# Convolution tail of a two-layer diffusion step: first chunk's norm between the other means, last adaLN group around it, second chunk's norm among the pointwise products

## The chip, the cores and the metric

The kernel runs on one core of one Trainium2 chip. The metric is the device time of one execution in microseconds (us). A core has five engines that run side by side, each through its own list of instructions in order: TensorE (PE; PEld is its weight load), VectorE (DVE), ScalarE (ACT), GpSimd (POOL) and SyncE (SP), which here issues nearly all transfers. An instruction that waits holds up all that stand behind it on its engine.

## The reference

One step of a hybrid backbone for 128 context tokens and 1024 noisy tokens, 1024 channels, two layers. Layer 0 mixes tokens by a convolution, layer 1 by attention; each is followed by a convolutional FFN.

```python
mod = (silu(cond) @ ada_w[i] + ada_b[i])                    # adaLN, per layer
sh1, sc1, g1, sh2, sc2, g2 = split(mod, 6)
h = modulate(rmsnorm(x, norm1_g[i]), sh1, sc1)
# layer 0, conformer_conv:
a, g = split(h @ w_pw1, 2);  u = a * sigmoid(g)
u = dwconv(u, dw_w, dw_b)                                   # 31 taps per channel
u = silu(layernorm(u, ln_g, ln_b))
y = u @ w_pw2
x = x + g1 * y
h = modulate(rmsnorm(x, norm2_g[i]), sh2, sc2)
x = x + g2 * conv_ffn(h, ...)
```

All is float32; each large product is made of three, with weights and activations split into a high and a low part.

## The kernel before

Channels lie on partitions, in 8 tiles (`KT`) of 128; the 1152 tokens lie along the free axis, in three chunks of 384 columns (`NCH`, index `c`). Only the stretch around the change is told here.

**Gate products and taps.** `gated(j, c)` makes channel tile `j` of the convolution's input `u`: two products (`ppa`, `ppg`) of 24 matmuls, a sigmoid, a multiplication. For tiles 0 to 6 the 31 taps are shared between VectorE (`taps_vector`, into the PSUM tile `da`) and ScalarE with GpSimd (`taps_pool`, into `pacc`); `join` adds the two into `U[c][:, j]`. For the last tile, `j = 7`, TensorE does 16 taps of each chunk with diagonal matrices (`taps_tensor`, into `dl`), VectorE adds seven more (`L660`) and GpSimd's eight join them (`L666`).

**Norm of a chunk.** `mean_head(c)` adds channel tiles 0 to 6 into the mean `mu` (seven matmuls, `L737`). `layer_norm(c)` is a generator, advanced a step at a time: the last matmul of the mean (`L744`), which needs the join of tile 7; two subtractions on VectorE (`L749`); squares on ScalarE (`lnsq`), summed on VectorE and GpSimd (`lnss`); six small matmuls that sum them over channels (`lnv`, `L325`); the reciprocal root on GpSimd (`lnv_r`); three matmuls that spread it over partitions (`L342`); then multiplications, SiLU and the split into `ln_h` and `ln_l`. `mu` of chunks 1 and 2, the norms' banks, `dl` and the products share PSUM tiles.

**adaLN.** `ada(pool, l, grp)` is a generator too. It reads 2048 columns of `ada_w` in 16 transfers of 512 KB ("halves" below, two to a step), each into one of three buffers `adaw`, and multiplies each by `cs` (`L270`, two matmuls of 512 columns that a trace shows as four). A row to SBUF by ScalarE (`adar`, `L279`), four transposes (`adat`) and additions into `mods` end a group. Group (1, 2) is the last of six; its result is not read before layer 1.

**Products.** `project_residual` runs for `c` = 0, 1, 2 over eight output tiles `m`: a product `pw2p` of 24 matmuls with weight tile `w16`, `w17`, ..., the residual on VectorE into `X[c]` (`L384`), a square on ScalarE. `X[c]` is read back from DRAM (`reload`, `L388`) into the buffer that `U[c]` held, so the transfer starts when the last `ln_l` of that chunk is written. `weights` keeps three raw tiles in flight and splits each on ScalarE (`w_hi`, `L220`) and VectorE (`w_lo`, `L221`).

**Order.** A scheduler orders the instructions of each engine, except where `manual_schedule` names an engine: there program order holds. SP is in program order everywhere. Before, VectorE and TensorE are in program order from the taps of tile 6 up to the end of the loop over the last taps, and the generators in `bg` (the adaLN groups, then the norms) advance one step per `tick()`.

Of the kernel before, what the change touches and what calls it, by code (L numbers as in the profile page):

```python
# [18 lines left out]
KT = D // P  # L19
# [4 lines left out]
NCH = NT // CH  # L24
# [55 lines left out]
def tile_hybrid_step(ctx: ExitStack, tc: tile.TileContext, a: dict, outs: list):  # L80
# [31 lines left out]
    def ntile(name, n=CH, dt=F32):  # L112
        return np_.tile([P, n], dt, tag="n", name=name)
# [30 lines left out]
    pool = Banks()  # L144


    bg = []

    def tick():
        for g in list(bg):  # L150
            if next(g, "end") == "end":
                bg.remove(g)
# [90 lines left out]
    weights = Weights()  # L243
# [8 lines left out]
    def ada(pool, l, grp):  # L252
        def load(kt):
            out = []
            for half in range(2):
                w = slot("adaw", f"adaw{l}_{grp}_{kt}_{half}")
                c0 = grp * 2048 + half * 1024
                nc.sync.dma_start(w, a["ada_w"][l, kt * P : (kt + 1) * P, c0 : c0 + 1024])
                out.append(w)
            return out  # L260

        nxt = load(0)
        yield
        ps = pool("ms", f"ada{l}_{grp}")
        for kt in range(KT):
            w = nxt
            if kt + 1 < KT:
                nxt = load(kt + 1)
            for q in range(4):
                nc.tensor.matmul(  # L270
                    ps[32 * q : 32 * q + 32, :],
                    cs[:, kt, :],
                    w[q // 2][:, (q % 2) * 512 : (q % 2) * 512 + 512],
                    start=(kt == 0),
                    stop=(kt == KT - 1),
                )
            yield
        row = slot("adaw", f"adar{l}_{grp}", n=512)
        nc.scalar.activation(row, ps, AF.Copy)  # L279
        yield  # L280
        pt = pool("ms", f"adat{l}_{grp}")
        for i in range(4):
            nc.tensor.transpose(pt[:, i * P : (i + 1) * P], row[:, i * P : (i + 1) * P], ident)
        ptv = pt.rearrange("p (i q c) -> p q i c", i=4, c=32)
        b0 = grp * 16
        for cond in range(2):
            nc.vector.tensor_tensor(
                mods[l][:, b0 : b0 + 16, cond].rearrange("p (q i) -> p q i", i=4),
                ptv[:, :, :, cond],
                adab[:, l * 48 + b0 : l * 48 + b0 + 16].rearrange("p (q i) -> p q i", i=4),  # L290
                ALU.add,
            )
        for n, gname in ((0, "norm1_g"), (1, "norm2_g")):
            v = 1 + 3 * n
            if v // 2 == grp:
                for cond in range(2):
                    nc.vector.scalar_tensor_tensor(
                        gsc[l][n][:, :, cond],
                        mods[l][:, v * 8 : v * 8 + 8, cond],
                        1.0,  # L300
                        cols(gname, l * KT, KT),
                        ALU.add,
                        ALU.mult,
                    )
# [172 lines left out]
    def chain(*gens):  # L477
        for g in gens:
            yield from g
# [25 lines left out]
    def cols(name, i, n):  # L505
        return vecs[:, at[name] + i : at[name] + i + n]
# [3 lines left out]
    slot = lambda tag, *args, **kw: (slot_0 if tag in ("adaw", "vrow") else slot_a)(tag, *args, **kw)  # L510
# [68 lines left out]
    us = []  # L579

    def gated(j, c):

        if c == 0:
            us.append((weights.take(min(j, 1)), weights.take(min(j, 1)), slot("u", f"u{j}")))
            for z in (0, NS + HALF, NT + 2 * HALF):
                nc.gpsimd.memset(us[j][2][:, z : z + HALF], 0.0)
        wa, wg, u = us[j]
        psa = project(pool, wa, H[c], f"ppa{j}_{c}")
        tick()
        psg = project(pool, wg, H[c], f"ppg{j}_{c}")  # L590
        yield
        tick()
        sg = ntile(f"sg{j}_{c}")
        nc.scalar.activation(sg, psg[:, 0:CH], AF.Sigmoid)
        for lo, hi, cond in pieces(c):
            o = HALF + c * CH + lo + HALF * cond
            nc.vector.tensor_tensor(u[:, o : o + hi - lo], psa[:, lo:hi], sg[:, lo:hi], ALU.mult)
        tick()
        if c == 1:
            weights.ahead(SPLITS, SPLITS)  # L600

    gate0 = []
# [31 lines left out]
    slot = lambda tag, *args, **kw: (slot_a if tag == "u" else slot_c)(tag, *args, **kw)  # L634

    U = [xtile(f"u_{c}") for c in range(NCH)]
    SPAN = [(0, CH), (CH, 2 * CH), (2 * CH, CONV_N)]

    def tap(j, t):
        return dww[:, j, t : t + 1]  # L640
# [12 lines left out]
    def taps_vector(j, u, d, n, s0_, s1_, fresh):  # L653

        for t in range(n):
            src = u[:, s0_ + t : s1_ + t]
            if t == 0 and fresh:
                nc.vector.tensor_scalar(d, src, tap(j, t), None, ALU.mult)
            else:
                nc.vector.scalar_tensor_tensor(d, src, tap(j, t), d, ALU.mult, ALU.add)  # L660
            yield
# [8 lines left out]
    last = KT - 1  # L670
    for j in range(last + 1):
        if j:
            for c in range(NCH):
                if j == 1:
                    nc.sync.dma_start(xs_d[0][:, c], X[c])
                for _ in gated(j, c):
                    pass
        if j == 1:
            bg.append(chain(*(ada(pool, l, g) for l, g in ((0, 1), (0, 2), (1, 0), (1, 1), (1, 2)))))
        if j == last:  # L680
            break
        u = us[j][2]
        da = pool("acc", f"da{j}")
        pacc = slot("pacc", f"pacc{j}")
        t0 = TAPS - (POOL_TAPS if j < last - 1 else POOL_TAPS_6)
        taps_pool(j, u, pacc, t0, 0, CONV_N)

        def on_vector(j=j, u=u, da=da, pacc=pacc, t0=t0):
            for _ in taps_vector(j, u, da[:, 0:CONV_N], t0, 0, CONV_N, True):
                pass  # L690
            for c in range(NCH):
                join(j, da, pacc, c)

        if j < last - 1:
            on_vector()
# [3 lines left out]
    u = us[last][2]  # L699
    t0 = TAPS - POOL_TAPS_7  # L700
    te = t0 - PE_TAPS
# [3 lines left out]
    dl = []  # L705

    def taps_tensor(c):
        s0_, s1_ = SPAN[c]
        dl.append(pool("mm", f"dl{c}")[:, 0 : s1_ - s0_])
        for i in range(PE_TAPS):  # L710
            t = te + i
            nc.tensor.matmul(
                dl[c], diag[:, i, :], u[:, s0_ + t : s1_ + t], start=(i == 0), stop=(i == PE_TAPS - 1)
            )


    vector = ExitStack()
    vector.enter_context(tc.manual_schedule(engines={mybir.EngineType.DVE, mybir.EngineType.PE}))
    on_vector()
    for c in range(NCH - 1):  # L720
        taps_tensor(c)

    L = [None] * NCH
# [3 lines left out]
    def mean_head(c):  # L727
        nonlocal mu_all
        if c == 0:
            mu = pool("mm", "mu0")  # L730
        else:
            if c == 1:
                mu_all = pool("acc", "mu").rearrange("p (c n) -> p c n", c=NCH)
            mu = mu_all[:, c]
        mus.append(mu[:, 0:CH])
        for j in range(last):
            nc.tensor.matmul(mus[c], mean_w, U[c][:, j, :], start=(j == 0), stop=False)  # L737
# [55 lines left out]
    pacc = slot("pacc", f"pacc{last}")  # L793
    for c in range(NCH):
        taps_pool(last, u, pacc, t0, *SPAN[c])
    for c in range(NCH):
        for _ in taps_vector(last, u, dl[c], te, *SPAN[c], False):
            tick()
        join(last, dl[c], pacc, c, SPAN[c][0])
        bg.append(layer_norm(c))  # L800
        if c == 0:
            tick()

            taps_tensor(NCH - 1)
            for i in range(1, NCH):
                mean_head(i)
    vector.close()

    def project_residual(H, X, c, acc, l, name, tag):
        for m in range(KT):  # L810
            w = weights.take()
            ps = project(pool, w, H[c], f"{name}p{c}_{m}")
            residual(ps, X, m, c, l, 2)
            add_stat(acc, m, c, X[c][:, m, :], tag=tag)
            tick()
# [4 lines left out]
    for c in range(NCH):  # L820
        while L[c] is None:
            tick()
        X[c] = reload(0, c, "x1_")
        project_residual(L, X, c, acc1, 0, "pw2", "tmp")
        bg.append(norm_mod(pool, X, acc1, c, 0, 1, H, "n1"))

    pool.open(mm=(5, 512), t=(2, 512), ms=(1, 512))
# [2 lines left out]
    sF, slot = phase(s=(6, NT), g=(4, NT + 3))  # L830
# [13 lines left out]
    sK, slot = phase(s=(4 * NKV, SLOT))  # L844
# [128 lines left out]
    for b in QKV_ORDER:  # L973
        ws = [weights.take(), weights.take()]
        for tt in range(NTT):
            c, t = divmod(tt, CH // P)
# [190 lines left out]
    for s in range(-3, len(steps)):  # L1167
# [4 lines left out]
        if s >= 0:  # L1172
            i, t = steps[s]
# [24 lines left out]
        if s >= 0:  # L1198
            probs.pop(s)
            i, t = steps[s]  # L1200
# [13 lines left out]
    sF, slot = phase(s=(6, NT), g=(4, NT + 3))  # L1214
# [94 lines left out]
```

## Time and profile before

| | |
|---|---|
| median of 3 runs | 2824.04 us (2820.50 to 2824.44) |
| profiled execution | 2820.44 us, of which the span is 2818.6 us |
| TensorE busy | 2722.3 us (97% of the span), 15959 matmuls |
| VectorE / ScalarE / GpSimd busy | 56% / 37% / 25% |
| mean granted TensorE clock | 0.989 |
| chain that ended last | TensorE 92%, VectorE 4%, ScalarE 1%, transfers 1% |

TensorE is busy nearly throughout, and in the page's 40 slices its share falls below nine tenths only in the first slice and in the sixth and seventh, 352 to 493 us. That is the stretch of the change; all times below are counted from the start of the span. The granted clock is given as a share of 2.4 GHz.

### The profile page before, as it was taken

The numbers are of one execution on the slowest core, as the hardware profiler recorded it, in microseconds if no ns is written. First come the engines' busy times: TensorE is split into PE (matmuls) and PEld (weight loads), VectorE is DVE, ScalarE is ACT, GpSimd is POOL, SyncE is SP. The second block draws the span as 40 slices with busy tenths as digits, with TensorE's granted clock in tenths as the row PEclk, the third lists the DMA queues.
The fourth block names the chain that finished last, engine by engine and source line by source line (L and its number), as shares of the span: only waits on it lengthen the run. The fifth ranks groups of instructions, "written<-read, shape, count | busy, mean of one in ns | idle before, by whom it ended". The sixth has DMA issues, their size and how long they took to land.

```text
span 2818.6 us, 40015 instructions
## 1 busy us (share of the span) xinstructions
PE 2722.3 (97%) x15959; PEld 2572.0 (91%) x15959; DVE 1584.7 (56%) x2747; ACT 1053.8 (37%) x2068; POOL 698.9 (25%) x782
## 2 busy tenths in 40 slices
PE   7999967999999999999999899999999999999999
PEld 4867637999999999999999789899999999999998
DVE  5878855644444444445653788867444444444445
ACT  5545534442222212212465677755422222222222
POOL 2777822400000000000555566535000000000003
PEclk9999988999999999999999999999999999999999
DMA  7465533411111111111120000034111111111111
GB/s 258 157 187 162 160 101 94 149 38 45 46 38 46 41 42 45 38 45 45 70 82 9 1 1 1 23 120 143 45 46 38 45 39 45 46 38 45 31 53 68
DMA packets 194419, 192.18 MB, mean 68 GB/s; under 512 B 7072, under 2 KB 173323, under 8 KB 192698
## 3 DMA queue, kind: packets, MB, share of 16 engines
q1 hardware_dynamic: 193946, 189.53, 21.5%
q8 instruction: 126, 2.06, 0.3%
q14 instruction: 59, 0.48, 0.1%
q0 software_dynamic: 288, 0.11, 0.0%
HBM read 175.19 MB, written 14.42 MB: 67 GB/s over the span
## 4 chain that ended last, share of the span: by engine, by line
PE 92%; DVE 4%; ACT 1%; DMA 1%; issue 1%; POOL 0%; SPq 0%; DVEq 0%; POOLq 0%; ACTq 0%
PE f1pd L249 3%; PE f1pd L247 3%; PE f1pd L248 3%; PE f0pg L249 3%; PE f1pg L249 3%; PE f1pg L248 3%; PE f0pg L248 3%; PE f0pv L248 3%; PE f1pg L247 3%; PE f1pv L248 3%; PE f1pv L247 3%; PE f0pg L247 3%; PE f0pv L247 3%; PE f1pv L249 3%; PE f0pv L249 3%; PE f0pd L247 3%
## 5 line engine op out<-in xcount | busy, mean ns | idle before, releaser
L220 ACT ACTIVATE w_hi<-w_raw 128x1024 fp32r<-128x1024 f32 x208 | 218.0, 1058 | 950.2 <-PE f0pd L248 223.7
L221 DVE TENSOR_TENSOR w_lo<-w_raw,w_hi 128x1024 fp32r<-128x1024 f32 x208 | 267.8, 1296 | 427.5 <-ACT w_hi L220 425.0
L651 POOL TENSOR_TENSOR pacc<-pacc,tmp 128x1167 f32<-128x1167 f32 (+2 forms) x98 | 234.2, 2392 | 63.4 <-ACT tmp L650 53.1
L384 DVE SCALAR_TENSOR_TENSOR x<-f1pd,mods,x 128x256 f32<-128x256 f32 (+1 forms) x352 | 170.1, 514 | 102.7 <-PE f1pd L249 102.5
L384 DVE SCALAR_TENSOR_TENSOR x<-f0pd,mods,x 128x256 f32<-128x256 f32 (+1 forms) x352 | 169.8, 514 | 99.1 <-PE f0pd L249 98.9
L660 DVE SCALAR_TENSOR_TENSOR da<-u,dww,da 128x1167 f32<-128x1167 f32 x126 | 180.9, 1436 | 3.1
L1117 POOL TENSOR_TENSOR pr<-pr,sm 128x384 f32<-128x384 f32 x192 | 153.8, 829 | 106.3 <-DVE sm L1115 52.1
L248 PE MATMUL f1pd<-f1al,w_hi 128*128 128x384 f32 x528 | 178.7, 338 | 0.0
L249 PE MATMUL f1pd<-f1ah,w_lo 128*128 128x384 f32 x528 | 178.6, 338 | 0.0
L249 PE MATMUL f0pd<-f0ah,w_lo 128*128 128x384 f32 x528 | 178.5, 338 | 0.0
L248 PE MATMUL f0pd<-f0al,w_hi 128*128 128x384 f32 x528 | 178.4, 338 | 0.0
L247 PE MATMUL f1pd<-f1ah,w_hi 128*128 128x384 f32 x528 | 178.4, 339 | 0.0
L411 POOL MEMSET f1gp<- 128x1 f32 x66 | 3.6, 98 | 703.8 <-DVE f1gp L435 665.7
L411 POOL MEMSET f0gp<- 128x1 f32 x66 | 3.6, 98 | 703.8 <-DVE f0gp L435 690.7
L247 PE MATMUL f0pd<-f0ah,w_hi 128*128 128x384 f32 x528 | 177.9, 338 | 0.0
L249 PE MATMUL f0pg<-n_h,w_lo 128*128 128x384 f32 x528 | 176.6, 334 | 0.0
L249 PE MATMUL f1pg<-n_h,w_lo 128*128 128x384 f32 x528 | 176.6, 334 | 0.0
L248 PE MATMUL f1pg<-n_l,w_hi 128*128 128x384 f32 x528 | 176.5, 334 | 0.0
L247 PE MATMUL f1pg<-n_h,w_hi 128*128 128x384 f32 x528 | 176.5, 334 | 0.0
L248 PE MATMUL f1pv<-n_l,w_hi 128*128 128x384 f32 x528 | 176.5, 334 | 0.0
L248 PE MATMUL f0pg<-n_l,w_hi 128*128 128x384 f32 x528 | 176.5, 334 | 0.0
L248 PE MATMUL f0pv<-n_l,w_hi 128*128 128x384 f32 x528 | 176.5, 334 | 0.0
(329 smaller groups left out, 7790.6 us busy)
## 6 DMA issues: line engine op xcount, KB each, us to landing
adaw<-in_ada_w_dram SPq DMA_DIRECT2D x96, 512.0 KB, 4.5
w_raw<-in_ffn_w_up_dram SPq DMA_DIRECT2D x88, 512.0 KB, 3.8
w_raw<-in_ffn_w_down_dram SPq DMA_DIRECT2D x44, 512.0 KB, 3.7
w_raw<-in_conv_w_pw_dram SPq DMA_DIRECT2D x40, 512.0 KB, 6.7
w_raw<-in_attn_w_o_dram SPq DMA_DIRECT2D x24, 512.0 KB, 4.3
xs_d<-x SPq DMA_DIRECT2D x6, 1536.0 KB, 11.1
x<-xs_d SPq DMA_DIRECT2D x6, 1536.0 KB, 8.5
w_raw<-in_attn_w_qkv_dram SPq DMA_DIRECT2D x12, 512.0 KB, 3.5
```

The source lines that it names most:

```text
L220: nc.scalar.activation(hi, raw, AF.Copy)
L221: nc.vector.tensor_tensor(lo, raw, raw32(hi), ALU.subtract)
L247: nc.tensor.matmul(ps, wh, mh, start=first, stop=False)
L248: nc.tensor.matmul(ps, wh, ml, start=False, stop=False)
L249: nc.tensor.matmul(ps, wl, mh, start=False, stop=last)
L384: nc.vector.scalar_tensor_tensor(xx, ps[:, lo:hi], mod(l, v, j, cond), xx, ALU.mult, ALU.add)
L411: nc.gpsimd.memset(gp[:, z : z + 1], 0.0)
L651: nc.gpsimd.tensor_tensor(d, d, tmp, ALU.add)
L660: nc.vector.scalar_tensor_tensor(d, src, tap(j, t), d, ALU.mult, ALU.add)
L1117: nc.gpsimd.tensor_tensor(pr[n], pr[n], ri.to_broadcast([P, CH]), ALU.mult)
```

## The change

The adaLN group (1, 2) leaves the background chain and is advanced by hand (`late`). The split of weight `w16` and the loads around it are placed by hand (`weights.ahead(1, 1)`), and the last gate tile no longer asks for it. The taps of TensorE are issued for all three chunks at once. A written list of steps replaces the ticks: the first chunk's norm (`norm0`) alternates with the second chunk's taps (`taps1`), the steps of `late` and the means of the other chunks. VectorE is in program order up to the end of that list, TensorE up to the end of the first chunk's eight products. The norms of chunks 1 and 2 go to the background as a chain, one step per `tick()` of the products.

```diff
-            us.append((weights.take(min(j, 1)), weights.take(min(j, 1)), slot("u", f"u{j}")))
+            us.append((weights.take(min(j, 1)), weights.take(int(0 < j < KT - 1)), slot("u", f"u{j}")))
...
-        if c == 1:
+        if c == 1 and j < KT - 1:
             weights.ahead(SPLITS, SPLITS)
...
-            bg.append(chain(*(ada(pool, l, g) for l, g in ((0, 1), (0, 2), (1, 0), (1, 1), (1, 2)))))
+            bg.append(chain(*(ada(pool, l, g) for l, g in ((0, 1), (0, 2), (1, 0), (1, 1)))))
+            late = ada(pool, 1, 2)
...
+    next(late)
     on_vector()
-    for c in range(NCH - 1):
+    for c in range(NCH):
         taps_tensor(c)
...
-    for c in range(NCH):
-        for _ in taps_vector(last, u, dl[c], te, *SPAN[c], False):
-            tick()
-        join(last, dl[c], pacc, c, SPAN[c][0])
-        bg.append(layer_norm(c))
-        if c == 0:
-            tick()
-
-            taps_tensor(NCH - 1)
-            for i in range(1, NCH):
-                mean_head(i)
-    vector.close()
+    def late_taps(c):
+        yield from taps_vector(last, u, dl[c], te, *SPAN[c], False)
+        join(last, dl[c], pacc, c, SPAN[c][0])
...
+    go(late_taps(0))
+    norm0, taps1 = layer_norm(0), late_taps(1)
+    go(norm0, 1)
+    go(late, 4)
+    for _ in range(2):
+        go(taps1, 1)
+        go(norm0, 1)
+    mean_head(1)
+    go(taps1, 2)
+    go(norm0, 1)
+    go(late, 2)
+    go(taps1, 1)
+    weights.ahead(1, 1)
+    go(norm0, 1)
+    mean_head(2)
+    go(norm0)
+    go(taps1)
+    go(late_taps(2))
+    go(late)
+    vector_by_hand.close()
+    bg.append(chain(layer_norm(1), layer_norm(2)))
...
         project_residual(L, X, c, acc1, 0, "pw2", "tmp")
+        if c == 0:
+            tensor_by_hand.close()
```

Here `go(gen, n)` advances a generator by `n` steps, or to its end.

On TensorE, between the first chunk's mean and the first product, stood before (`mu_2901` is chunk 0's mean, `u_822` and `u_823` are `U` of chunks 1 and 2, `lnv_3040` and `lnv_3104` the norms' banks of chunks 0 and 1):

```order
L744 MATMUL mu_2901<-u_821,mean_w 128x384
L712 MATMUL dl_2989<-u_2622,diag 128x399 x16
L737 MATMUL mu<-u_822,mean_w 128x384 x7
L737 MATMUL mu<-u_823,mean_w 128x384 x7
L325 MATMUL lnv_3040<-ones,lnss_0_3024 128x1
...
L342 MATMUL lnv_3040<-ident,lnv_r 128x128 x3
L744 MATMUL mu<-u_822,mean_w 128x384
L325 MATMUL lnv_3104<-ones,lnss_0_3088 128x1
L247 MATMUL pw2p_0_3147<-ln_h,w_hi 128x384
```

And now, from the taps of chunk 2 on (`lnv_2993` is chunk 0's norm, `ada_2_2932` the last adaLN group):

```order
L713 MATMUL dl_2827<-u_2581,diag 128x399 x16
L742 MATMUL mu_2844<-u_821,mean_w 128x384 x7
L749 MATMUL mu_2844<-u_821,mean_w 128x384
L270 MATMUL ada_2_2932<-adaw_2_0_0_2766,cs 32x512 x2
...
L742 MATMUL mu<-u_822,mean_w 128x384 x7
L325 MATMUL lnv_2993<-ones,lnss_0_2968 128x1
...
L270 MATMUL ada_2_2932<-adaw_2_5_1_3006,cs 32x512 x2
L342 MATMUL lnv_2993<-ident,lnv_r 128x128 x3
L742 MATMUL mu<-u_823,mean_w 128x384 x7
...
L270 MATMUL ada_2_2932<-adaw_2_7_1_3069,cs 32x512 x2
L283 MATMUL adat_2_3081<-ident,adar_2_3079 128x128 x4
```

The taps of chunk 2 stand ahead of chunk 0's mean, the adaLN halves stand in three groups (eight, four, four) behind the mean and on both sides of the spread, and chunk 1's mean and sums no longer stand ahead of the first product: its last matmul comes after product `m = 0`, its sums after `m = 3`, its spread after `m = 4`, and chunk 2's last matmul of the mean after `m = 6`.

On VectorE, after chunk 1's join, stood before:

```order
L660 SCALAR_TENSOR_TENSOR dl_2989<-u_2622,dww,dl_2989 128x399
L749 TENSOR_TENSOR u_822<-u_822,mu 128x1536 x2
L660 SCALAR_TENSOR_TENSOR dl_2989<-u_2622,dww,dl_2989 128x399
L761 TENSOR_TENSOR lnss_0_3088<-lnsq_0_0_3086 128x384
L660 SCALAR_TENSOR_TENSOR dl_2989<-u_2622,dww,dl_2989 128x399
L764 TENSOR_TENSOR lnss_0_3088<-lnss_0_3088,lnsq_0_1_3095 128x384 x2
```

And stands now (`x_0_3092` is `X[0]`, read back from DRAM):

```order
L660 SCALAR_TENSOR_TENSOR dl_2827<-u_2581,dww,dl_2827 128x399 x6
L384 SCALAR_TENSOR_TENSOR x_0_3092<-pw2p_0_3100,mods_95,x_0_3092 128x384
L660 SCALAR_TENSOR_TENSOR dl_2827<-u_2581,dww,dl_2827 128x399
L754 TENSOR_TENSOR u_822<-u_822,mu 128x1536 x2
L666 TENSOR_TENSOR u_823<-dl_2827,pacc_2852 128x256
L666 TENSOR_TENSOR u_823<-dl_2827,pacc_2852 128x128
L287 TENSOR_TENSOR mods_96<-adat_2_3081,adab 128x16 x2
L221 TENSOR_TENSOR w_lo<-w_raw,w_hi 128x1024
L384 SCALAR_TENSOR_TENSOR x_0_3092<-pw2p_1_3138,mods_95,x_0_3092 128x384
```

The residual of the first product, which needs the transfer of `X[0]`, now stands ahead of chunk 1's subtraction, and both ahead of the low part of the fourth product's weights.

## Rows read from the trace of the kernel before

**Rows 1.** Windows of the stretch: busy us (instructions) per engine, granted clock, transfers.

```profile
core 0: us, PE busy (x) PEld busy (x) DVE busy (x) ACT busy (x) POOL busy (x), PEclk, DMA share, GB/s
...
362.00:382.00 20.00, 13.78 (x51) 4.68 (x50) 12.50 (x21) 6.83 (x10) 8.60 (x7) 1.00 0.64 204
...
405.00:426.30 21.30, 1.99 (x4) 0.87 (x4) 16.56 (x21) 11.53 (x16) 1.58 (x2) 0.55 0.45 138
426.30:447.20 20.90, 20.86 (x114) 20.54 (x113) 10.11 (x13) 8.00 (x11) 3.29 (x4) 0.89 0.24 69
447.20:465.00 17.80, 2.07 (x4) 0.93 (x5) 11.22 (x13) 9.02 (x12) 2.58 (x3) 0.62 0.17 50
465.00:485.30 20.30, 20.30 (x114) 20.30 (x115) 8.93 (x9) 8.04 (x13) 6.33 (x6) 0.92 0.39 130
485.30:520.00 34.70, 34.70 (x206) 34.70 (x206) 26.49 (x32) 21.79 (x34) 17.45 (x13) 1.00 0.50 160
```

**Rows 2.** Waits of TensorE, 362 to 485 us: total us, times, longest.

```profile
PE mu L744 <- DVE u L666: 23.1, 3, 12.6
PE lnv L325 <- DVE lnss L764: 14.2, 2, 7.6
```

**Rows 3.** TensorE in order of time: start, us, instruction [idle before, releaser].

```profile
332.22 3.39 PE L712 MATMUL dl<-u,diag 128*128 128x384 f32 x10
...
373.79 1.05 PE L270 MATMUL ada<-adaw,cs 128*32 128x512 f32 x4 [1.40 <-DMA adaw<-in_ada_w_dram]
...
378.10 0.66 PE L283 MATMUL adat<-ident,adar 128*128 128x128 f32 x4 [0.70 <-ACT adar L279]
380.97 0.91 PE L744 MATMUL mu<-u,mean_w 128*128 128x384 f32 x2 [2.22 <-DVE u L666]
381.72 10.89 PE L712 MATMUL dl<-u,diag 128*128 128x399 f32 x32
392.45 9.19 PE L737 MATMUL mu<-u,mean_w 128*128 128x384 f32 x28
401.48 1.40 PE L325 MATMUL lnv<-ones,lnss 128*128 128x1 f32 x12
404.07 0.93 PE L342 MATMUL lnv<-ident,lnv_r 128*128 128x128 f32 x6 [1.19 <-POOL lnv_r L334]
417.64 1.65 PE L744 MATMUL mu<-u,mean_w 128*128 128x384 f32 x2 [12.64 <-DVE u L666]
425.96 0.56 PE L325 MATMUL lnv<-ones,lnss 128*128 128x1 f32 x2 [6.67 <-DVE lnss L764]
...
455.35 1.65 PE L744 MATMUL mu<-u,mean_w 128*128 128x384 f32 x2 [8.19 <-DVE u L666]
...
480.98 0.34 PE L247 MATMUL pw2p<-ln_h,w_hi 128*128 128x384 f32 x1
...
485.14 0.34 PE L247 MATMUL pw2p<-ln_h,w_hi 128*128 128x384 f32 x1
```

**Rows 4.** Tile `adaw`, 290 to 380 us: its 512 KB loads, issue to landing.

```profile
DMA to landing us min/median/max: 3.5/4.8/7.8
```

**Rows 5.** VectorE in order of time, same columns.

```profile
336.52 23.55 DVE L660 SCALAR_TENSOR_TENSOR da<-u,dww,da 128x1167 f32<-128x1167 f32 x16
365.79 1.23 DVE L221 TENSOR_TENSOR w_lo<-w_raw,w_hi 128x1024 fp32r<-128x1024 f32 x1 [5.72 <-ACT w_hi L220]
...
373.19 3.25 DVE L660 SCALAR_TENSOR_TENSOR dl<-u,dww,dl 128x384 f32<-128x384 f32 x5
...
415.43 0.96 DVE L790 TENSOR_TENSOR ln_l<-u,ln_h 128x768 fp32r<-128x768 f32 x1 [1.11 <-ACT ln_h L781]
...
419.33 3.42 DVE L749 TENSOR_TENSOR u<-u,mu 128x1536 f32<-128x1536 f32 x2 [1.20 <-PE mu L744]
```

**Rows 6.** GpSimd in order of time, the sums of chunk 1's squares.

```profile
425.71 2.07 POOL L764 TENSOR_TENSOR lnss<-lnss,lnsq 128x384 f32<-128x384 f32 x2 [0.95 <-ACT lnsq L758]
```

**Rows 7.** Tile `xs_d`, 360 to 600 us: the three 1.5 MB reloads, issue to landing.

```profile
DMA to landing us min/median/max: 6.1/9.2/9.3
```

More of the change, by code (lines that the diff above doesn't have):

```diff
@@ L714, in taps_tensor @@
             )
-    vector = ExitStack()
-    vector.enter_context(tc.manual_schedule(engines={mybir.EngineType.DVE, mybir.EngineType.PE}))
+    assert not bg
+    tensor_by_hand, vector_by_hand = ExitStack(), ExitStack()
+    tensor_by_hand.enter_context(tc.manual_schedule(engines={mybir.EngineType.PE}))
+    vector_by_hand.enter_context(tc.manual_schedule(engines={mybir.EngineType.DVE}))
+    next(late)
     on_vector()
-    for c in range(NCH - 1):
+    for c in range(NCH):
         taps_tensor(c)
@@ L795, in tile_hybrid_step, with go @@
         taps_pool(last, u, pacc, t0, *SPAN[c])
-    for c in range(NCH):
-        for _ in taps_vector(last, u, dl[c], te, *SPAN[c], False):
-            tick()
+    def late_taps(c):
+        yield from taps_vector(last, u, dl[c], te, *SPAN[c], False)
         join(last, dl[c], pacc, c, SPAN[c][0])
-        bg.append(layer_norm(c))
-        if c == 0:
-            tick()
-            taps_tensor(NCH - 1)
-            for i in range(1, NCH):
-                mean_head(i)
-    vector.close()
+    def go(gen, n=None):
+        while n is None or n > 0:
+            if next(gen, "end") == "end":
+                return
+            n = n and n - 1
+    go(late_taps(0))
[19 more added lines that the diff above has]
+    bg.append(chain(layer_norm(1), layer_norm(2)))
     def project_residual(H, X, c, acc, l, name, tag):
```

## The prediction, made before the result was known

> **What bounds the kernel now.** I read the page first: TensorE is busy 97% of the span and makes 92% of the chain that ended last, so only a stretch in which it stands idle has anything to give. The page's slices show one such stretch, and the windows size it [rows 1]: from 362 to 485.3 us TensorE waits, mostly in two holes, 405 to 426.3 (2.0 of 21.3 us busy) and 447.2 to 465 (2.1 of 17.8). From 485.3 on it is full. The waits name what ends them [rows 2]: 23.1 us for the join of the last channel tile (the last matmul of a mean), 14.2 us for the sums of squares. The order of time [rows 3] shows why. After chunk 0's spread at 404.07 the next TensorE instruction is chunk 1's last mean matmul (12.64 us of waiting), then chunk 1's sums (6.67); the first product starts behind them, at 426.5, although it needs chunk 0 alone. The same comes back for chunk 2 at 455.35 (8.19). The granted clock falls in both holes, to means of 0.55 and 0.62, so TensorE resumes at the lower of its levels, 1.2 instead of 2.4 GHz: four products took the window of 20.9 us [rows 1], where four of 4.16 us (480.98 to 485.14, 24 matmuls at full clock [rows 3]) and about 2 us of small matmuls are 18.6.
>
> **The change, part by part.** The place from which both orders run alike is the first tap matmul at 332.22, the place at which TensorE is full again the first product of chunk 1, 485.14 before [rows 3]. I lay the new TensorE order end to end between them.
>
> Taps and first mean. 48 tap matmuls without adaLN between them are three times 10.9 us [rows 3]: 332.2 to 364.8. Seven mean matmuls follow, half of the 9.19 us that fourteen took: 369.4. The last one needs VectorE: the sixteen taps end at 360.1, the last tile's taps began at 373.2 [rows 5], and of these 13.1 us a wait of 5.72 for a weight and two splits of about 1.2 leave the path, so they begin at 365.0; seven at 0.65 are 4.6, a join 0.6: 370.2. ScalarE splits two weights sooner, ahead of GpSimd's taps; these are ready well before the join. The mean ends at 371.1 instead of 381.9.
>
> The last adaLN group. It is 16 halves of 1.05 us on TensorE; before, it ran among the taps and ended with 1.40 us waits for its loads [rows 3]. Now eight stand between the mean and chunk 1's mean matmuls, and everything behind a half waits with it. Three buffers are full at the start; each later half needs a load that is issued when the half three places earlier ends. For a load I take the median of 4.8 us; the bounds are 3.5 and 7.8 [rows 4]. Three halves end at 374.2; the fourth lands at 372.1 + 4.8 = 376.9, the seventh, issued when the fourth ends at 378.0, at 382.8, and the eighth ends at 384.9. Of these 13.8 us 5.4 are waiting. Mean 4.6 and sums 1.4 [rows 3]: 390.9. The sums of squares were ready long before (before, 8.5 us after the mean's end, [rows 5, 6] for chunk 1), so the loads set the pace here. Three halves, then the wait for the load issued at 391.9, one half: 397.8; spread 0.9: 398.7, against 405.0 before. Mean of chunk 2: 403.3. Three halves, a load issued at 404.4, one half: 410.2; ScalarE's row 0.7, transposes 0.66 [rows 3]: the first product starts at 411.6, 14.9 us sooner. ScalarE has that row ahead of its last `ln_h`, so the last `ln_l` (0.96 [rows 5]) ends at about 412.7.
>
> A rule of the Trainium skill speaks against this piece. In 362 to 382, where halves alternated with waits for loads, TensorE was busy 13.8 of 20 us and the granted clock stayed at 1.00, the upper level [rows 1]. The skill (TensorE: Matmul & The Clock Gate, HAM oscillation) says that short runs of matmuls behind waits for transfers let the clock drop, so that each run begins slow. By the row the first product costs 4.2 us; by the rule some 2 us more, as in the window after 426.3.
>
> Products of chunk 0. Chunk 1's mean (0.9) comes after `m = 0`; `m = 0` to `2` run without a reload: 425.0. The reload of `X[0]` starts at 412.7 and takes 9.2 us [rows 7]: 421.9. On VectorE the first residual waits for it, and behind it stand a tap, chunk 1's subtraction (3.42 [rows 5]), a join and the low part of the weight of `m = 3`: 0.6 + 0.6 + 3.4 + 0.6 + 0.3 + 1.2 = 6.7, so 428.7. Product `m = 3` therefore loses 3.4 us and ends at 432.5. Next on TensorE are chunk 1's sums. Undisturbed they were ready 8.5 us after the subtraction began (419.33 to 427.78 [rows 5, 6]); now two weight splits and two squares lie between on ScalarE, and additions on GpSimd, for which I add 5 us: 423.1 + 13.5 = 436.6, a new wait of 4.1. With sums 1.4, spread 0.9, the last mean matmul of chunk 2 (0.9) and four products the chunk ends at 456.5. Chunk 1's second `ln_l` half stands behind chunk 2's subtraction on VectorE (452.4 + 3.4 + 1.7): 457.6.
>
> So chunk 1 begins 27.5 us sooner. Two waits follow that the trace of before does not have. Chunk 2's sums stand after two products of chunk 1, and on VectorE behind the residual that needs the reload of `X[1]`, which starts when `ln_l` ends (459.3 + 9.2, then 1.2): 469.7 against 466.6, 3.1 us. The reload of `X[2]` now starts after chunk 1's last residual, 2.3 + 9.2 us behind the last product; three products cover 12.5, then the weight of `m = 3` needs 3: 2.0 us. Neither can be a gain. The few rows that change places later, around two softmax steps of layer 1, I cost at nothing: TensorE's order there is unchanged.
>
> **The sum:** 27.5 - 3.1 - 2.0 = 22.4 us. Against the profiled execution's 2820.4 that gives 2798.0; that execution is among the faster, 3.6 below the median of the three, so medians compare at 2798 to 2801.6. I take 2800. For the bounds: with loads of 3.5 us the four that lie on the path each give 1.3 back, and without the waits in the products another 13.7 come back, 41 us in all; with loads of 7.8 us the four cost 12 more and two slow starts as after the holes (2.3 each) 4.6, which leaves 6 us. A loss needs the clock, rival E.
>
> **Rivals.** A, the forecast: both holes become short waits, gain 15 to 30 us, 2794 to 2809. Chance 0.62.
>
> B, the waits in the products vanish as well: reloads nearer 6.1 us [rows 7], so that `m = 3` and chunk 2's sums come without waiting, and the interleaved squares cost nothing. That is 3.4 + 4.1 + 1.1 + 3.1 + 2.0, less what stays for other reasons: gain 30 to 40, 2784 to 2794. For it: three products cover 12.5 us of a reload. Against: 9.2 is the median and 9.3 the longest, so two of three were that long. Chance 0.15.
>
> C, the loads bind harder: the halves' loads take up to 7.8 us, and the first product starts at 420 or later, held by an adaLN result that nobody reads yet; gain 6 to 15, 2809 to 2818. For it: these loads held TensorE before as well (1.40 us at 373.79), and three buffers allow no more. Against: the median of 4.8 us lies nearer the shortest. Chance 0.13.
>
> D, the saving returns whole as waits at the places above and the result lies within 0.2%, which is 5.6 us and about what a measurement of this kernel can tell from no change. A's waits in the products would have to be more than twice as long. Chance 0.05.
>
> E, slower: the clock. A product at 1.2 GHz lasts up to twice its 4.16 us. If the new short waits (3.4, 4.1, 1.1, 3.1 us) keep the clock down through most of the 24 products, from six slow products on the 22 us are gone; with sixteen slow it is 67 - 22 = 45 us slower, 2869. For it: the clock did fall in the two holes. Against: after each hole it was back within a window whose mean is 0.89 and 0.92 [rows 1], and waits of 1 to 2 us in 362 to 382 did not move it. The skill's rule named above would say the same as this rival if the products were cut into short runs; here a run between waits is 8 us or more. Chance 0.05. That the change does not do what it says I rule out: the order of both engines shows it.
>
> **The numbers.** Predicted 2800 us. Low 2786 reaches well into B, high 2812 into C; about 2 in 10 lie outside, D and E among them. Faster by over 0.2%: A, B and C, 0.90; within: 0.05; slower: 0.05.
>
> **What would show it.** In the changed profile the last mean matmul of chunk 0 ends near 371; the chain from there to the first product alternates adaLN halves with loads, and the first product starts near 412; TensorE's waits name `adaw` loads with some 15 us in all, while the two rows of `mu` and `lnv` shrink from 37 to under 10 us; the clock is at 1.00 from 371 to 412. Chunk 1's first product starts near 458. I am wrong if the products of chunk 0 show the low clock for more than one product, if a reload holds more than 8 us at one place, or if the first product starts after 420.

## The result, and the profile after

The changed kernel takes 2804.19 us (median of three runs, 2803.43 to 2806.16) against 2824.04: a ratio of 0.9935, with a 95% interval of 0.9912 to 0.9957. Timed again beside two experiments, in five rounds, it had 2806.40 us and a ratio of 0.9941 (0.9928 to 0.9955). The prediction was 2800 us, in a range of 2786 to 2812. The profiled span went from 2818.6 to 2801.7 us.

The order of time of TensorE in the changed kernel, with the columns of [rows 3], shows the stretch from the first tap matmul to the last product's last matmul.

```profile
331.92 31.54 PE L713 MATMUL dl<-u,diag 128*128 128x384 f32 x96
...
368.76 0.91 PE L749 MATMUL mu<-u,mean_w 128*128 128x384 f32 x2 [0.78 <-DVE u L666]
369.60 1.91 PE L270 MATMUL ada<-adaw,cs 128*32 128x512 f32 x12
375.14 1.05 PE L270 MATMUL ada<-adaw,cs 128*32 128x512 f32 x4 [3.63 <-DMA adaw<-in_ada_w_dram]
...
390.22 1.40 PE L325 MATMUL lnv<-ones,lnss 128*128 128x1 f32 x12
...
396.98 1.92 PE L270 MATMUL ada<-adaw,cs 128*32 128x512 f32 x4 [3.53 <-DMA adaw<-in_ada_w_dram]
398.83 1.59 PE L342 MATMUL lnv<-ident,lnv_r 128*128 128x128 f32 x6
...
412.12 0.67 PE L247 MATMUL pw2p<-ln_h,w_hi 128*128 128x384 f32 x1
...
419.10 0.63 PE L247 MATMUL pw2p<-ln_h,w_hi 128*128 128x384 f32 x1
...
437.34 2.29 PE L325 MATMUL lnv<-ones,lnss 128*128 128x1 f32 x10 [2.20 <-POOL lnss L769]
439.49 0.67 PE L247 MATMUL pw2p<-ln_h,w_hi 128*128 128x384 f32 x1
...
459.94 0.51 PE L247 MATMUL pw2p<-ln_h,w_hi 128*128 128x384 f32 x2
...
499.45 0.33 PE L247 MATMUL pw2p<-ln_h,w_hi 128*128 128x384 f32 x1
...
538.33 0.33 PE L249 MATMUL pw2p<-ln_h,w_lo 128*128 128x384 f32 x1
```

The same last matmul in the kernel before, from its own order of time:

```profile
554.27 0.33 PE L249 MATMUL pw2p<-ln_h,w_lo 128*128 128x384 f32 x1
```

Three readings. First, chunk 0's spread is done near 400.4, the first product starts at 412.12 (426.4 before) and chunk 1's first product at 459.94 (485.14, [rows 3]). Second, from the first tap matmul to the last product's last matmul it is 538.33 - 331.92 = 206.4 us, against 554.27 - 332.22 = 222.1: 15.6 of the 16.9 us of the span lie here, 0.3 ahead of it and 1.0 behind. This length is called the stretch below; it leaves out the few us by which profiled executions differ before it. A profiled execution is one of the timed runs and need not be a middle one: for the changed kernel, e1, e7 and e11 it is the fastest of its runs, for e4, e6, e8 and e10 the slowest. Third, the records of the products say how long one took: 419.10 - 412.12 less 0.35 for a mean matmul between them is 6.6 us for the first product, where a product at full clock takes 4.16.

The page's row of slices for the kernel before has one more slice under nine tenths than was said ahead of the prediction, the 23rd (1550 to 1621 us); it stands at eight tenths in the changed kernel as well, and no part of the change lies there.

The waits of TensorE, 362 to 540 us (total us, times, longest):

```profile
PE ada L270 <- DMA adaw<-in_ada_w_dram: 12.5, 6, 3.6
PE lnv L325 <- DVE lnss L769: 3.4, 2, 2.5
PE lnv L325 <- POOL lnss L769: 2.2, 1, 2.2
PE pw2p L249 <- DVE w_lo L221: 2.1, 1, 2.1
PE pw2p L248 <- DVE ln_l L793: 1.5, 1, 1.5
```

The two large rows of [rows 2], 23.1 and 14.2 us, have shrunk to 0.8 us (`mu`) and 5.6 us (`lnv`); waits for the loads of `adaw` stand in their place. The windows, with the columns of [rows 1], show what these do:

```profile
371.50:400.00 28.50, 18.82 (x69) 7.13 (x68) 9.51 (x13) 4.66 (x5) 3.84 (x4) 0.82 0.63 204
400.00:412.00 12.00, 8.51 (x36) 3.93 (x35) 6.33 (x7) 8.61 (x13) 0.00 (x0) 0.93 0.26 86
412.00:419.00 7.00, 7.00 (x28) 6.94 (x27) 6.41 (x10) 0.03 (x1) 0.00 (x0) 0.62 0.71 248
419.00:432.10 13.10, 13.04 (x74) 12.51 (x72) 11.03 (x16) 6.22 (x9) 3.58 (x3) 1.00 0.70 188
432.10:446.70 14.60, 9.95 (x42) 9.87 (x43) 3.68 (x6) 3.58 (x5) 5.97 (x5) 0.65 0.25 74
...
460.00:499.40 39.40, 36.98 (x223) 36.58 (x222) 30.62 (x34) 25.65 (x38) 16.29 (x15) 1.00 0.50 147
499.40:538.40 39.00, 36.54 (x206) 35.89 (x205) 32.32 (x43) 20.55 (x33) 20.37 (x15) 0.96 0.55 163
```

The granted clock is 0.82 in the mean from 371.5 to 400 and 0.62 while the first product runs; it falls again behind the waits for chunk 1's sums (0.65). The halves' loads, and below them the three reloads, issue to landing (the longest of the three, 7.0, is that of `X[0]`):

```profile
DMA to landing us min/median/max: 3.6/4.4/4.8
```

```profile
DMA to landing us min/median/max: 6.3/6.3/7.0
```

### The profile page after: what moved, and what is told of

Its sections match the earlier page's. It is cut to its first block, busy times and chain, and to the rows that moved or that the text cites. A ratio compares the mean times of both kernels' runs of the same rounds, so it can differ in the third digit from the quotient of the medians.

```text
span 2801.7 us, 40014 instructions
## 1 busy us (share of the span) xinstructions
PE 2726.4 (97%) x15959; PEld 2579.7 (92%) x15959; DVE 1586.9 (57%) x2747; ACT 1053.6 (38%) x2068; POOL 697.7 (25%) x782
## 4 chain that ended last, share of the span: by engine, by line
PE 90%; DVE 5%; DMA 2%; ACT 1%; issue 1%; POOL 0%; SPq 0%; DVEq 0%; ACTq 0%; POOLq 0%
PE f1pd L247 3%; PE f1pd L249 3%; PE f1pd L248 3%; PE f1pg L249 3%; PE f0pg L249 3%; PE f0pg L247 3%; PE f0pv L249 3%; PE f1pv L249 3%; PE f1pg L248 3%; PE f1pg L247 3%; PE f1pv L248 3%; PE f0pg L248 3%; PE f0pv L247 3%; PE f0pv L248 3%; PE f1pv L247 3%; PE f0pd L248 3%
## 5 line engine op out<-in xcount | busy, mean ns | idle before, releaser
L247 PE MATMUL f0pg<-n_h,w_hi 128*128 128x384 f32 x528 | 176.5, 334 | 0.0
```

The lines of the kernel that those rows point to most:

```text
L247: nc.tensor.matmul(ps, wh, mh, start=first, stop=False)
```

## The experiments

All times are medians; ratios are to the kernel before on the same chip, with 95% intervals. The last column is the stretch in the profiled execution of each.

| kernel | us | ratio | stretch us |
|---|---|---|---|
| before | 2821.9 to 2824.8 | 1 | 222.1 |
| changed | 2804.19, again 2806.40 | 0.9935, 0.9941 | 206.4, 207.4 |
| e1, chunk 1's norm ahead of the products | 2817.85 | 0.9980 (0.9970 to 0.9990) | 216.7 |
| e2, only the first two loads of the last adaLN group | 2786.95 | 0.9867 (0.9851 to 0.9882) | 186.0 |
| e3, last group among the taps | 2801.00 | 0.9916 (0.9903 to 0.9928) | 203.1 |
| e4, last group among the products | 2787.35 | 0.9869 (0.9854 to 0.9884) | 188.1 |
| e5, spare matmuls in the load waits | 2802.76 | 0.9921 (0.9908 to 0.9934) | 203.0 |
| e6, chunks 1 and 2 among the products alone | 2810.96 | 0.9946 (0.9931 to 0.9961) | 210.4 |
| e7, e4 with its gaps filled | 2789.74 | 0.9876 (0.9863 to 0.9889) | 187.0 |
| e8, e7 with the next norm handed out | 2787.75 | 0.9866 (0.9852 to 0.9881) | 189.7 |
| e10, e3 with a later row | 2796.88 | 0.9907 (0.9893 to 0.9922) | 196.7 |
| e11, e4 with the next norm later | 2782.35 | 0.9856 (0.9842 to 0.9869) | 182.0 |

**The parts of the change: e1, e6, e3, e10.**

```diff
 e1, against the changed kernel
+    go(layer_norm(1))
     vector_by_hand.close()
-    bg.append(chain(layer_norm(1), layer_norm(2)))
+    bg.append(layer_norm(2))
```

> One part undone: chunk 1's whole norm stands by hand ahead of chunk 0's first product again; the rest is as in the changed kernel. Theory (products of chunk 0 gained because they no longer stand behind chunk 1's mean and statistics): the first product starts some 16 us later (near 428, from 412.1), of which about 2 us of sums and spread, 4.7 us of waits for the sums (2.51 + 2.20) and 3 to 4 us at the lower clock come back inside the products; net 6 to 9 us slower than the changed kernel, 2810 to 2813. Rival (the wait for chunk 1's statistics only changes places): within 3 us of the changed kernel, 2801 to 2807.

TensorE of e1 in order of time:

```profile
410.24 1.65 PE L749 MATMUL mu<-u,mean_w 128*128 128x384 f32 x2 [2.46 <-DVE u L666]
422.26 0.59 PE L325 MATMUL lnv<-ones,lnss 128*128 128x1 f32 x2 [10.38 <-DVE lnss L769]
...
429.06 0.67 PE L247 MATMUL pw2p<-ln_h,w_hi 128*128 128x384 f32 x1
```

The direction was right and the size too small: the stretch is 10.3 us longer, and by the ratios 0.4% or 11 to 13 us go. The mean and the sums of chunk 1 hold TensorE for 2.46 and 10.38 us, and the first product comes 18.0 us later, counted from the first tap. Little of this came back among the products of chunk 0, as chunk 2's sums then make the wait (6.64 us) that chunk 1's had made.

```diff
 e6, against the kernel before (TensorE's order by hand up to the end of chunk 0's products)
         join(last, dl[c], pacc, c, SPAN[c][0])
-        bg.append(layer_norm(c))
         if c == 0:
+            bg.append(layer_norm(c))
             tick()
 ...
+    bg.append(chain(layer_norm(1), layer_norm(2)))
```

> The kernel before with one part of the change alone: the norms of chunks 1 and 2 go in the background among the products, TensorE's order is still by hand to the end of chunk 0; the last adaLN group stays among the taps and chunk 0's statistics stay behind the means of chunks 1 and 2. Theory (this part is what gains; e1 lost 13.7 of the 19.8 us without it, and e3 lost nothing without the spread group): spread of chunk 0 at 404 as before, first product from about 409 and bounded by the last ln_l near 418, 14 to 20 us faster than before, within 4 us of the changed kernel. Rival (the parts need each other: without the earlier statistics the products begin too late for chunk 1's norm to matter): gain under 8 us against before.

The theory holds with less than it asked: 13.9 us by the medians, 15 by the ratio and 11.7 of the stretch, where 14 to 20 were expected, and not within 4 us of the changed kernel. Its six runs lie 13 us apart (2801.78 to 2815.11). Its TensorE waits after the spread for ScalarE's first `ln_h`, as everything of chunk 0 is still late:

```profile
411.93 1.27 PE L342 MATMUL lnv<-ident,lnv_r 128*128 128x128 f32 x6 [1.19 <-POOL lnv_r L334]
417.51 0.69 PE L247 MATMUL pw2p<-ln_h,w_hi 128*128 128x384 f32 x1 [4.31 <-ACT ln_h L782]
```

In this execution the clock also fell at a place where it stayed up in the kernel before: behind the wait ahead of chunk 0's last mean matmul, which is 2.22 us long in both ([rows 3], 380.97).

```profile
385.87 1.65 PE L745 MATMUL mu<-u,mean_w 128*128 128x384 f32 x2 [2.22 <-DVE u L666]
```

```profile
386.00:388.00 2.00, 2.00 (x4) 1.06 (x5) 0.45 (x1) 0.00 (x0) 0.00 (x0) 0.50 0.00 0
```

From there to the end of the means of chunks 1 and 2 it needs 23.5 us, where the kernel before needs 20.5 (380.97 to 401.48): some 3 us of e6's stretch are the clock.

```diff
 e3, against the changed kernel (e10: the last steps behind chunk 0's subtraction instead)
             nc.tensor.matmul(dl[c], diag[:, i, :], ...)
+            if (c * PE_TAPS + i) % 6 == 5:
+                next(late)
 ...
+    next(late)
     mean_head(0)
+    next(late, None)
 ...
-    go(late, 4)
-    go(late, 2)
-    go(late)
```

> One part undone: the last adaLN group stands among the tap matmuls of the last channel tile, a step after every sixth, as such groups did before; the norm order of the changed kernel stays. Theory (the group costs its 16.8 us of TensorE time anywhere, and between the statistics its load waits and the low clock on top): chunk 0's mean ends near 386.5, means and sums to 397.5, spread to 400.6, first product bounded by the last ln_l near 413 but at full clock; 3 to 6 us faster than the changed kernel, 2798 to 2801. Rival (spreading the group around the statistics is what gained, since it fills waits that are there anyway): slower than the changed kernel by 4 us or more, 2808 and above.

> e3 again (the last adaLN group among the taps), with the group's transposes and VectorE's additions behind chunk 0's subtraction instead of ahead of the last tile's VectorE taps, which had cost e3 a wait of 5.7 us of its own. Theory (the place between the statistics costs more than e3 showed): chunk 0's mean ends near 380 instead of 386; 3 to 6 us faster than e3, 5 to 9 faster than the changed kernel, 2795 to 2799. Rival (the statistics are bound by other work of VectorE, and the 5.7 us only change places): within 2 us of e3, 2799 to 2803.

e3 shortens the stretch by 3.3 us, as the theory said, though its interval and that of the changed kernel overlap. It carried a fault of its own: TensorE waits 5.69 us for the join of the last tile, whose taps stood on VectorE behind the additions of the group's result. e10 takes that away, and was timed beside the changed kernel: 9.5 us faster, and the intervals (0.9893 to 0.9922, 0.9928 to 0.9955) are apart. TensorE of e10 in order of time:

```profile
383.07 0.81 PE L752 MATMUL mu<-u,mean_w 128*128 128x384 f32 x2
...
390.82 0.38 PE L325 MATMUL lnv<-ones,lnss 128*128 128x1 f32 x2 [1.98 <-DVE lnss L772]
...
404.14 0.64 PE L247 MATMUL pw2p<-ln_h,w_hi 128*128 128x384 f32 x1
```

The mean ends at 383.9, which is 47.1 us after the first tap matmul (336.80 there) and 9.3 later than in the changed kernel, since the group stands ahead of it. Yet the first product starts 67.3 us after the first tap matmul, where the changed kernel needs 80.2. So the three parts can be priced by the stretch, one after the other: chunk 1's and 2's norms among the products -11.7 (222.1 to 210.4, e6), chunk 0's statistics among the means -13.6 (to 196.7, e10), the last adaLN group spread around them +9.7 (to 206.4). The sum is the 15.6 us of the result. The split between the first two is good to some 3 us only, by the clock that fell in e6; by the ratios the three are -15, -11 and +10 us. The second part holds the new place of the tap matmuls and of weight `w16`'s split as well, and no run tells these apart. But the sign of the third is clear: e10 and the changed kernel differ in the place of the group alone. One of the three parts works against the other two.

**What the spread group costs: e2 and e5.**

```diff
 e2, against the changed kernel
         def load(kt):
+            if few and kt:
+                return nxt
```

> The order of the changed kernel, but the last adaLN group loads its first two half tiles only and multiplies with these throughout, so 14 loads of 512 KB are left out (the group's result is not the reference's). Theory (the loads of adaw bind from 371 to 412): the 12.5 us of waits go, the granted clock stays at 1.00 there, the first product starts near 399.5 instead of 412.1 and takes 4.2 us instead of 6.6; 12 to 16 us faster than the changed kernel, 2788 to 2792. Rival (the statistics on VectorE, ScalarE and GpSimd set the pace and the loads only fill their time): waits named lnss, lnv_r or ln_l take their place, gain under 5 us, above 2799.

e2's order of time and one window:

```profile
371.70 3.64 PE L272 MATMUL ada<-adaw,cs 128*32 128x512 f32 x32
...
391.81 0.42 PE L247 MATMUL pw2p<-ln_h,w_hi 128*128 128x384 f32 x1
```

```profile
371.50:391.80 20.30, 19.44 (x115) 9.58 (x115) 14.96 (x19) 9.29 (x13) 3.84 (x4) 1.00 0.00 1
```

The loads bind, and more than forecast: the stretch is 20.4 us shorter than in the changed kernel, of which only 12.5 are named as waits for `adaw`. Two things are in the rest, and e2 doesn't part them (e5 prices the first). The clock stays at 1.00 there. And eight halves take 3.64 us when nothing holds them, 0.46 each, where the prediction had 1.05; so 16 are some 7.4 us, and not the 16.8 of e3's expectation. A half fills two of the four blocks of 32 partitions of its PSUM tile, and two halves that follow each other, which fill all four, run side by side. The kernel before shows it: two halves take 1.07 us there, and one that stands alone takes 1.05.

```profile
335.54 1.07 PE L270 MATMUL ada<-adaw,cs 128*32 128x512 f32 x8
```

The next bound shows too, as the rival had it in part: the wait for chunk 1's sums grows to 6.24 us, from 2.51 + 2.20 in the changed kernel.

```diff
 e5, against the changed kernel
+    def fill(i):
+        for _ in range({3: 5, 6: 1, 7: 2, 11: 5, 15: 4, 16: 1}.get(i, 0)):
+            nc.tensor.matmul(mu_all[:, 0, 0:CH], mean_w, U[2][:, 0, :], start=True, stop=True)
 ...
                 if fill and q % 2 == 0:
+                    fill(2 * kt + q // 2)
```

> The changed kernel with 18 spare matmuls of 128x384 (0.65 us each, a sum that nobody reads) put into TensorE's waits between the halves of the last adaLN group: five before the 4th half, one before the 7th, two before the 8th, five before the 12th, four before the 16th, one before the transposes. Theory (TensorE's short waits let the granted clock fall, and the fall costs the mean of chunk 1 1.0 us, a half 0.9, the spread 0.7, the first product 2.5): clock near 1.00 from 371 to 419, first product in 4.2 us, 4 to 6 us faster than the changed kernel, 2798 to 2800. Rival (the lower clock lies inside the waits for loads and costs nothing, or the spare matmuls run over): within 2 us of it, 2802 to 2806, or slower.

Its windows, the starts of its first product and of chunk 1's, and two rows of its waits:

```profile
371.50:400.00 28.50, 27.31 (x112) 11.98 (x107) 12.76 (x16) 5.15 (x6) 3.86 (x4) 1.00 0.68 215
...
410.00:420.00 10.00, 10.00 (x57) 9.73 (x57) 9.65 (x13) 0.90 (x2) 0.00 (x0) 1.00 0.85 266
```

```profile
409.73 0.42 PE L247 MATMUL pw2p<-ln_h,w_hi 128*128 128x384 f32 x1
...
455.35 0.51 PE L247 MATMUL pw2p<-ln_h,w_hi 128*128 128x384 f32 x2
```

```profile
PE pw2p L249 <- DVE w_lo L221: 4.5, 1, 4.5
...
PE ada L272 <- DMA adaw<-in_ada_w_dram: 1.2, 4, 0.5
```

With work in the waits the clock stays at 1.00 from 371.5 to 420. Counted from the first tap matmul (333.68 there) the first product starts 4.1 us sooner than in the changed kernel (76.1 against 80.2), the second 6.5 sooner, chunk 1 6.3 sooner. Spare matmuls can only add work, so this is what the low clock had cost at least, as the theory had it. But chunk 2 starts 1.0 later, since the last product of chunk 1 waits 4.46 us for `w_lo`, and of the 6.3 us 3.4 are left at the end. By time e5 and the changed kernel can't be told apart; the places can.

**Where the group is better put: e4, e7, e8, e11.**

```diff
 e4, against the changed kernel
     go(norm0, 1)
-    go(late, 4)
+    mean_head(1)
 ...
-    mean_head(1)
+    mean_head(2)
 ...
-    go(late, 2)
+    go(late, 1)
 ...
-    mean_head(2)
+    go(late, 1)
 ...
-    go(late)
 ...
             tick()
+            if l == 0 and c == 0:
+                next(late, None)
```

> A candidate: chunk 0's statistics beside the means of chunks 1 and 2, and of the last adaLN group only two of eight steps there; the other six stand one behind each of chunk 0's products. Theory (adaLN is not needed until layer 1, and one step per product never waits for its load and fills the wait for chunk 1's sums): sums of chunk 0 end near 380.5, spread 383.7, first product starts 389 to 393 (412.1 in the changed kernel), 12.6 us of adaLN come back inside chunk 0, the 4.7 us of waits for chunk 1's sums and 3.5 us at the lower clock go; 12 to 17 us faster than the changed kernel, 2787 to 2792. Rival (the reload of X[0] and the adaw loads collide, or VectorE's residuals become the bound): new waits of 8 us or more in chunk 0, gain under 5 us, above 2799.

The theory held: 188.1 us of stretch, nearly that of e2 although all loads are made. One step behind each product waits 1.5 us for its loads in all, and the sums of chunk 1 wait 0.56 us. What binds now is the norm of chunk 0: the first product waits 2.07 us for `ln_h` and takes 9.1 us.

```diff
 e7, against e4 (the sums and the spread are the two go(norm0, 1) behind the loop;
 mean_head(c, j0, j1) adds channel tiles j0 up to j1)
+    go(late, 1)
     mean_head(1)
 ...
-    mean_head(2)
+    mean_head(2, 0, 3)
+    weights.ahead(3, 1)
-    go(taps1, 2)
     go(norm0, 1)
-    go(late, 1)
-    go(taps1, 1)
-    weights.ahead(1, 1)
+    mean_head(2, 3, 5)
+    go(taps1, 3)
     go(norm0, 1)
+    mean_head(2, 5, last)
     go(late, 1)
```

> The candidate of e4 with its idle places before the first product filled: the first adaLN step ahead of chunk 1's mean (so that the next loads land in time), chunk 2's mean split in 3 + 2 + 2 matmuls around the sums and the spread, and three weights split on VectorE before the sums instead of between the spread and its first multiplication. Theory (e4 still loses 1.9 us to the splits, 2.1 to a load, 2.1 to ln_h and 3 at the lower clock here): first product some 2 us sooner and no low clock before it; 3 to 5 us faster than e4, 2782 to 2785. Rival (chunk 0's first product is bound by the last ln_l, and that chain by ScalarE): within 1.5 us of e4.

Nothing was gained, as the rival had it: the median is 2.4 us above that of e4, and the intervals overlap. GpSimd's last sum of squares takes the place of the load (2.7 us), and the first product is bound by `ln_h` and `ln_l`, for which it waits twice and four times.

```diff
 e8, against e7, in norm_mod's loop over tiles
+            if name == "n1" and c < NCH - 1 and j % 2:
+                yield
```

> e7 with one more edit: the norm of chunks 0 and 1 after the products is handed out two tiles at a time over the next products instead of eight at once. Theory (chunk 2's first product waits 2.1 us for the low part of its weight, w_lo, which stands on VectorE behind that norm, and not for the reload of X[2]): the waits of 2.1 and 0.4 us and the low clock behind them go; 2 to 4 us faster than e7. Rival (the weight itself comes late, since its load stands behind the reload on SyncE's queue): the wait stays, within 1 us of e7.

e8 tells nothing about its question: the trace has VectorE's instructions around chunk 2's first product in the order of e7, and the wait of 2.1 us for `w_lo` is as before.

```diff
 e11, against e4
-        bg.append(norm_mod(pool, X, acc1, c, 0, 1, H, "n1"))
+        if c == 1:
+            bg.append(chain(*(norm_mod(pool, X, acc1, i, 0, 1, H, "n1") for i in range(2))))
+        if c == 2:
+            bg.append(norm_mod(pool, X, acc1, c, 0, 1, H, "n1"))
```

> e4 with the norms of chunks 0 and 1 that follow the products both started after chunk 1's products, so that VectorE has 8 us less to do in chunk 1. Theory (chunk 2's first product waits for w_lo, 2.1 us and 0.4 for w_hi, since VectorE is full there with chunk 0's next norm and chunk 2's own; e8 could not show it, as its edit left the order of VectorE as it was): these waits and the low clock behind them go; 2 to 5 us faster than e4, 2782 to 2785. Rival (the reload of X[2] and the weights behind it on SyncE's queue set the pace, or the norms come back as a wait at the FFN): within 1.5 us of e4, or slower.

VectorE of the changed kernel ahead of chunk 2's first product (499.45), and of e11 ahead of its own (479.27):

```profile
494.92 2.58 DVE L793 TENSOR_TENSOR ln_l<-u,ln_h 128x1536 fp32r<-128x1536 f32 x1
...
497.95 0.60 DVE L356 SCALAR_TENSOR_TENSOR n_u<-x,gsc,n_b 128x384 f32<-128x384 f32 x1
...
500.22 0.84 DVE L364 SCALAR_TENSOR_TENSOR n_l<-n_u,mods,n_h 128x384 fp32r<-128x384 f32 x1
500.98 2.01 DVE L221 TENSOR_TENSOR w_lo<-w_raw,w_hi 128x1024 fp32r<-128x1024 f32 x1
```

```profile
475.50 0.61 DVE L384 SCALAR_TENSOR_TENSOR x<-pw2p,mods,x 128x384 f32<-128x384 f32 x1
476.03 1.51 DVE L221 TENSOR_TENSOR w_lo<-w_raw,w_hi 128x1024 fp32r<-128x1024 f32 x1
477.47 1.75 DVE L793 TENSOR_TENSOR ln_l<-u,ln_h 128x1536 fp32r<-128x1536 f32 x1
```

The window of chunk 2's products in e11:

```profile
479.20:514.50 35.30, 35.30 (x212) 35.30 (x211) 32.86 (x50) 23.80 (x40) 21.46 (x17) 1.00 0.61 179
```

In the changed kernel `w_lo` stands behind six us of unbroken work, the `n_u` and `n_l` of chunk 0's next norm among it, and comes when the product already waits. In e11 it is done at 477.5, before the product starts, and the waits for `w_hi` and `w_lo` are gone; so is the low clock behind them (1.00, against 0.96 from 499.4 to 538.4 in the changed kernel). That gives 6.1 us of stretch against e4 and 5.0 by the medians, with intervals that overlap. e11 is the fastest of all, 1.4% under the kernel before. The changed kernel was repeated beside it and e10:

> The changed kernel itself, beside the two that follow on the same chip. Expected 2802 to 2806; from the first tap matmul of the last channel tile to the last product 206 us within 2.

It came out at 2806.40 us, 0.4 over what was expected, with 207.4 us of stretch, so the stretch repeats within 1 us here.

## Why the prediction was right, and where its steps were not

The time and the mechanism came out as forecast: rival A held, both holes became short waits. By its steps, in order:

- **Taps and first mean: right.** The mean ends at 369.7 (forecast 371.1); VectorE began the last tile's taps 1.5 us sooner than I had it.
- **The last adaLN group: right times, wrong reasons.** Sums end at 391.6 (390.9), spread at 400.4 (398.7), first product at 412.12 (411.6), and TensorE waits 12.5 us for loads (some 15 were named, though the working gives 5.4 + 2.7 + 2.7 = 10.8). The loads took 4.4 us in the median (4.8). But a half was taken at 1.05 us instead of the 0.46 that e2 shows. The sum did not suffer only because loads set the pace. The trace of before had the answer, eight matmul records in 1.07 us where a lone group of four shows 1.05; I read the lone one.
- **The clock: wrong.** Forecast was 1.00 from 371 to 412. It was 0.82 from 371.5 to 400, and the first product took 6.6 us, 2.4 over the 4.16. I had argued from [rows 1], where waits of up to 1.4 us between halves did not move the clock; here they were up to 3.63 us. e5 shows the cause: the same order with work in the waits keeps 1.00. The rule of the Trainium skill that I set aside says that runs of matmuls that are cut by waits for transfers each begin slow (TensorE: Matmul & The Clock Gate, HAM oscillation). The trace agrees with it: the first product lost 2.4 us.
- **Products of chunk 0: one wait too many, one right, one clock missed.** The 3.4 us at `m = 3` did not come, for two reasons: the reload of `X[0]` took 7.0 us, not 9.2 ([rows 7] has 6.1 to 9.3), so that the weight was ready at 426.4 and not at 428.7, and `m = 3` began at 427.4 and not at 425.0, since the first product was slow. That is the one wait by which rival B was right, and in part by luck. The wait for chunk 1's sums was 2.51 + 2.20 = 4.7 us (4.1), and GpSimd's additions end it. The clock fell behind it, so the fifth product took 6.6 us as well. The prediction called itself wrong if more than one product of chunk 0 showed the low clock, and two did: by that sign its account of the clock failed. The cost stayed far from rival E, as each slow stretch ended within one product. Chunk 1 starts 128.0 us after the first tap (forecast 457.6 - 332.2 = 125.4).
- **Chunks 1 and 2: mis-sized, 9.3 us for 5.1.** Chunk 1 takes 39.5 us from its first product to chunk 2's (34.65 before), chunk 2 38.9 (34.5). Here stands a fault of the sum itself: chunk 2's sums and spread moved from chunk 0's products into chunk 1's, 2.0 us (1.17 + 0.83), and were counted at nothing. The wait for `ln_l` (1.54) fell inside chunk 1 too; the wait of 3.1 for chunk 2's sums was 0.9. And the 2.0 us in chunk 2 were right in size alone: they lay at its first product, not at `m = 3`, and VectorE's order made them, not the reload of `X[2]`, whose issue at 505.2 comes after. e11 shows that. The low clock behind this wait (0.96 over the 39 us) is most of the rest.

So 22.4 us were forecast for the stretch and 15.6 came: 2.6 were lost up to chunk 1 and 4.2 in chunks 1 and 2. That 2800 lies only 4 us under the result is luck in part: the medians of the first runs differ by 19.8 us, more than the profiled spans, where the repeat beside e10 gave 15.5, and in the sum a wait that did not come stands against a clock that was not foreseen. What the prediction did not see at all is that the three parts pull apart. It priced the group's load waits between the statistics, but not the same group at another place. e10 has the same statistics without it, and is 9.5 us faster.

## What to carry to other kernels

Work that nobody needs soon belongs where each step meets its own load, one per product here (e4), and not between the links of a chain that everything waits for: there every load that is late is paid in full, with a slow start of the next matmuls on top. When a wait is moved, count what moves with it into the stretch that was full before (2.0 us of sums and spread here), and price the engine that prepares the operands there, as VectorE did for `w_lo`. Read the duration of a short instruction from a row in which several follow each other.

## What the hardware showed beyond that

- The granted clock fell to its lower level, 1.2 GHz, behind waits of 3.63, 3.53 and 2.80 us that had a few us of matmuls between them. The length of one wait does not tell it: a wait of 2.22 us left the clock at 1.00 in the kernel before and was followed by 0.50 in e6. With matmuls whose results nobody reads in these waits it stayed at 2.4 GHz (e5), and chunk 1 began 6.3 us sooner.
- Matmuls with 32 columns of weights that go to different blocks run side by side: two halves take 1.07 us, one 1.05, and eight (32 records) 3.64. The mean matmuls, with 128 columns of weights, take 4.68 us for 14 records of 384 columns; by that pace 32 records of 512 columns one after another would take some 14 us (an estimate). The Trainium skill (TensorEngine Tiling (Array Packing), Tiling Modes) says that the array can be split into four tiles of 32 columns that run matmuls at the same time. The trace agrees, and shows what that does to the record of a half read alone.
